# Two transformer layers and a gated block on one core: idle products at the start, modulation steps in other places, cross products of an inverse by halves

## The chip, the cores and the metric

The kernel runs on one core of a Trainium2 chip. The metric is the device time of one execution in microseconds; the kernel before has a median of 1013.92 over three runs (1012.06 to 1015.05). The engines are TensorE (PE, with its weight loads as PEld), VectorE (DVE), ScalarE (ACT), GpSimd (POOL) and SyncE (SP), which issues nearly all transfers.

## The reference, cut to what matters

Width 1024, 256 tokens, all in float32. A gated-linear-attention layer and an attention layer, each followed by a feed-forward with a convolution over three tokens, and then a block with a convolution branch, an RWKV-7 branch and a modulation by a vector c.

```python
def first_block(x, ...):
    for i in range(2):
        h = rmsnorm(x, norm_mix[i])
        x = x + (gla_mixer(h, ...) if i == 0 else attn_mixer(h, ...))
        x = x + conv_ffn(rmsnorm(x, norm_ffn[i]), w_up[i], w_conv[i], b_conv[i], w_down[i])
    return x

def gla_mixer(h, w_in, w_gate_up_f, ...):
    q, k, v, g, r = split(h @ w_in)                 # r: two ranks of 16 for the decays
    ...
    return (rmsnorm(o) * silu(g)) @ w_out

def conv_ffn(h, w_up, w_conv, b_conv, w_down):
    val, gate = split(depthwise_conv3(h @ w_up) + b_conv)
    return (silu(gate) * val) @ w_down

def second_block(x, c, ...):
    shift, scale, gate = split(silu(c) @ ada_w + ada_b)
    h = rmsnorm(x, norm_g) * (1 + scale) + shift
    c_val, c_gate, c_og, ts, r_og, g_conv, g_rwkv = split(h @ w_in)
    y_conv = silu(layernorm(conv31(c_val * sigmoid(c_gate)))) * silu(c_og) @ w_conv_out
    y_rwkv = rwkv7(ts, r_og)                        # state update by token, computed in chunks of 64
    m = sigmoid(g_conv) * y_conv + sigmoid(g_rwkv) * y_rwkv
    x = x + gate * (m @ w_out)
    return rmsnorm(x, final_g)
```

## The kernel before

Activations lie with the 1024 features on partitions, as 8 slices of 128 by 256 tokens. Each float32 matrix product is made of parts: ScalarE casts a weight slab of 128x1024 to its upper part hi (L78), VectorE subtracts it for the lower part lo (L80), and TensorE runs three products for each slice of 128 (mm3, L113 to L115), or one of width 512 over both parts of the activation and one of width 256 with the weight's lower part (mm2, L120 and L123). The weights come through SyncE's queue into a ring of five tiles `raw`; the tiles `adaw` of the modulation are in the same ring, so that a load waits until the tile five places earlier has been used up.

A list scheduler fixes each engine's order when the kernel is built; at run time an engine takes its instructions in that order and waits where an input is missing.

The stages are: gla (rank product `gr`, keys `pj`, queries, values, gates, output), ffn0, attn, ffn1 and second. The places that matter here:

- *Start.* `gla` makes the scaled activation (`ph_g`, `pl_g`), the rank product `gr` (64x256, eight slices), the column sums for the mean square (`rstd_cols`, L157, tile `nps_g`), then the key projection, four slabs of 24 products. `spread` (tile `rps_g`) brings the reciprocal root to all partitions. The products `lg` for the decays follow the keys. Ahead of all stand WARM products of 128x128 on ones (`warm`, L1331).
- *Modulation.* `ada` (L601) is a generator of 24 steps, eight for each third e of the modulation vector. One step loads 512 KB of `ada_w` into `adaw` and multiplies and adds it on VectorE into `ada` (L611, L613); the eighth also runs 16 small matmul rows `adaps` (L617) and an addition (L618). The table AD (L591) says how many steps are taken at each of the eight calls in gla (g), ffn0 (f0), attention (a) and ffn1 (f1).
- *Feed-forward.* For 22 pairs of slabs: up products, three-token convolution in `y` (L257 to L259), silu, product with the value (L263) and split into `gg` (ScalarE L130, VectorE L131). Then eight down products `dn` of 22 slices and their additions to x (L276).
- *Attention.* Keys are normed, turned (rope, L479 to L483) and transposed (`kTp`); queries follow; scores are reduced (mx, L568), exponentiated, scaled (rs, p, L574 and L577) and transposed (`pps`).
- *Inverse.* In `inv` the triangular inverse's diagonal blocks X are found by VectorE, which transposes them (X2 by halves at L869, all at L871); ScalarE copies the diagonal blocks into TT (L874); the cross blocks are products of 32x32, `zp` (L882) and `xp` (L892), copied at L885 and L895. `fill` puts products of other projections between them. Then `chain` follows the state over four chunks (`u`, `sp`, `op`).
- *End.* Conv branch: 31 taps on VectorE (L1081), normed into `yc`. `gated` projections give m and its parts `mh`; `wout` (L1122) multiplies by w_out with `project_both` and adds to x (L1131, twice for each slab, for the two parts of the activation); `final` (L1142) makes the last norm: squares on ScalarE, column sums, a square root that needs a table on ScalarE (loaded at L143), and four output pieces.

Of the kernel before, what the change touches and what calls it, by code (L numbers as in the profile page):

```python
# [10 lines left out]
F32 = mybir.dt.float32  # L11
# [6 lines left out]
P = 128  # L18
# [138 lines left out]
def rstd_cols(g, acc, name, eps=EPS):  # L157

    ps = g.ps.tile([P, 512], F32, name=f"nps_{name}")
    for t in range(2):  # L160
        for a in acc:
            g.nc.tensor.matmul(ps[:, 2 * t:2 * t + 2], a[:, t * P:(t + 1) * P], g.ones[:, :2], start=a is acc[0], stop=a is acc[-1])
    return rsqrt(g, ps[:, :4], 1.0 / D, eps, name)
# [134 lines left out]
def project(*a, **k):  # L298
    for _ in projecting(*a, **k):
        pass  # L300
# [45 lines left out]
def gla(g):  # L346
# [10 lines left out]
    for k in range(KD):  # L357
        mm3(nc, ps[:64, :T], (wh[:, k, :], wl[:, k, :]), (h[0][:, k, :], h[1][:, k, :]), k == 0, k == KD - 1)
    for d in range(2):
        rows = slice(32 * d, 32 * d + 16)  # L360
        nc.vector.tensor_tensor(out=rT[rows, :], in0=ps[rows, :T], in1=rstd[rows, :], op=ALU.mult)
# [229 lines left out]
AD = dict(zip(("g", "f0", "a", "f1"), "11111111,11111111,11111111,00000000".split(",")))  # L591
# [54 lines left out]
def second(g, order):  # L646
# [196 lines left out]
    def inv():  # L843
# [33 lines left out]
        for b in range(2):  # L877
            zp = psum.tile([P, 16, 32], F32, name=f"zp{b}")
            for i in range(16):
                for hf in range(2):  # L880
                    o = 64 * hf + 32
                    nc.tensor.matmul(zp[o:o + 32, i, :], Lb[64:96, hf, b, i, 32:], X2[64:96, hf, 16 * b + i, :], start=True, stop=True)  # L882
            for hf in range(2):
                o = 64 * hf + 32
                nc.scalar.copy(zt[o:o + 32, 16 * b:16 * b + 16, :], zp[o:o + 32])  # L885
            fill(1)
# [105 lines left out]
    def kept(name, src, f):  # L992
# [14 lines left out]
        def get(j):  # L1007
            t = sb.tile([P, T], F32, tag=name + "i", name=f"{name}i{j}")
            g.w.after(t, d[:, j, :])
            nc.scalar.activation(t, t, f)  # L1010
            return t
# [113 lines left out]
    def wout():  # L1125
        g.x = full("x2")
        g.w.after(g.x, g.xs)

        def ev(j, ps):
            for b in range(2):  # L1130
                nc.vector.scalar_tensor_tensor(out=g.x[:, j, :], in0=ps[:, b], scalar=g.mod[:, 16 + j:17 + j], in1=g.x[:, j, :], op0=ALU.mult, op1=ALU.add)  # L1131

        project_both(g, I["w_out"], v.mh, ev)
# [7 lines left out]
def final(g):  # L1141
# [8 lines left out]
    for a, n in ((0, 1), (1, 2), (3, 3), (6, 2)):  # L1150
# [144 lines left out]
def body(nc, tc, I, O, stages=("gla", "ffn0", "attn", "ffn1", "second")):  # L1295
    with ExitStack() as es:
# [33 lines left out]
        for _ in range(WARM):  # L1330
            nc.tensor.matmul(warm, g.ones, g.ones, start=True, stop=True)  # L1331
# [45 lines left out]
```

## Time and profile before

| | us |
|---|---|
| median of three runs | 1013.92 (1012.06 to 1015.05) |
| the profiled execution | 1013.54 |
| its span | 1011.7 |
| TensorE busy | 974.7 |
| VectorE busy | 832.3 |
| ScalarE busy | 611.0 |
| GpSimd busy | 5.1 |
| mean granted clock of TensorE | 0.983 |

The profile is of one execution. The span runs from its first to its last recorded instruction; 1.8 us of the profiled execution's time lie outside it. Busy times of engines overlap. Matmul ends are modelled: a product of width 256 is shown as about 0.28 us long although the next begins 0.12 us after it, so starts are read for the rate and not durations. The granted clock is a share of full speed, 2.4 GHz; the lower level, 1.2 GHz, shows as 0.5, and a stretch in between has held both.

### The profile page before, as it was taken

The page shows a single profiled execution, that of the slowest core. Times are in us where ns is not written, and L with a number is a line of the kernel's source. Part 1 is how long each engine was busy: PE and PEld are TensorE (multiplying, and loading weights), DVE is VectorE, ACT ScalarE, POOL GpSimd, SP SyncE. Part 2 cuts the span into 40 slices and gives each one's busy share as a digit, 9 for nine tenths or more (in the row PEclk, how much of TensorE's full clock was granted, in tenths as well). Part 3 has the DMA queues.
Part 4 walks back from the last instruction along what each step waited for, and adds up shares of the span by engine and source line. Part 5 has one row for each costly group of instructions (what it writes and reads, how often), then busy time and mean ns, then how long its engine had stood idle before and what let it go on. Part 6 is the DMA issues. An engine that isn't in the chain of part 4 may idle for free.

```text
span 1011.7 us, 19352 instructions
## 1 busy us (share of the span) xinstructions
PE 974.7 (96%) x7636; PEld 905.8 (90%) x7636; DVE 832.3 (82%) x1529; ACT 611.0 (60%) x1052; POOL 5.1 (0%) x15
## 2 busy tenths in 40 slices
PE   8999999999999999999999999999999999999796
PEld 7988899999888877999999889999988998898795
DVE  5956589888867886998888667999899898889795
ACT  6635666666544567676666456545676646745663
POOL 0000000000000000000000000000000000000000
PEclk8999999999999999999999999999999998999898
DMA  7738155556776861546656675455432362436451
GB/s 267 256 122 277 50 182 187 188 178 190 223 219 217 276 215 42 180 157 218 180 183 174 188 249 199 149 187 180 157 106 84 93 222 92 154 115 199 162 161 42
DMA packets 54442, 175.01 MB, mean 173 GB/s; under 512 B 6320, under 2 KB 12976, under 8 KB 53968
## 3 DMA queue, kind: packets, MB, share of 16 engines
q1 hardware_dynamic: 50464, 169.51, 52.7%
q10 hardware_dynamic: 3888, 4.27, 1.2%
q8 instruction: 60, 0.98, 0.4%
q14 instruction: 30, 0.25, 0.1%
HBM read 168.51 MB, written 5.24 MB: 172 GB/s over the span
## 4 chain that ended last, share of the span: by engine, by line
PE 79%; DVE 10%; DMA 4%; ACT 4%; issue 2%; ACTq 0%; DVEq 0%; SPq 0%
PE pj L113 8%; PE pj L115 8%; PE pj L114 8%; PE dn L120 8%; PE up L114 7%; PE up L115 7%; PE up L113 7%; PE pj L120 4%; PE dn L123 4%; DVE lo L80 3%; PE pj L123 2%; DMA adaw<-ada_w 2%; PE pt L113 2%; PE pt L114 2%; PE pt L115 2%
## 5 line engine op out<-in xcount | busy, mean ns | idle before, releaser
L78 ACT CAST hi<-raw 128x1024 fp32r<-128x1024 f32 (+2 forms) x286 | 295.0, 1034 | 243.2 <-PE pj L114 82.6
L80 DVE TENSOR_TENSOR lo<-raw,hi 128x1024 fp32r<-128x1024 f32 (+2 forms) x286 | 344.0, 1205 | 78.3 <-ACT hi L78 70.7
L114 PE MATMUL up<-h_f,hi 128*128 128x256 f32 x640 | 181.4, 284 | 0.5 <-DVE h_f L131 0.5
L113 PE MATMUL up<-h_f,hi 128*128 128x256 f32 x640 | 180.8, 283 | 0.3 <-ACT h_f L130 0.3
L115 PE MATMUL up<-h_f,lo 128*128 128x256 f32 x640 | 180.8, 283 | 0.0
L115 PE MATMUL pj<-h_s,lo 128*128 128x256 f32 x544 | 156.1, 287 | 1.7 <-DVE lo L80 1.7
L113 PE MATMUL pj<-h_s,hi 128*128 128x256 f32 x544 | 157.4, 290 | 0.0
L114 PE MATMUL pj<-h_s,hi 128*128 128x256 f32 x544 | 156.2, 287 | 0.0
L120 PE MATMUL dn<-gg,hi 128*128 128x512 f32 x352 | 124.9, 402 | 0.0
L114 PEld LDWEIGHTS up<-h_f,hi 128*128 128x128 f32 x640 | 122.8, 192 | 1.1 <-DVE h_f L131 1.1
L113 PEld LDWEIGHTS up<-h_f,hi 128*128 128x128 f32 x640 | 122.6, 192 | 0.5 <-ACT h_f L130 0.5
L115 PEld LDWEIGHTS up<-h_f,lo 128*128 128x128 f32 x640 | 122.8, 192 | 0.0
L115 PEld LDWEIGHTS pj<-h_s,lo 128*128 128x128 f32 x544 | 104.8, 193 | 2.6 <-DVE lo L80 1.9
L113 PEld LDWEIGHTS pj<-h_s,hi 128*128 128x128 f32 x544 | 104.9, 193 | 1.5
L114 PEld LDWEIGHTS pj<-h_s,hi 128*128 128x128 f32 x544 | 104.9, 193 | 1.1 <-issue 0.3
L1081 DVE SCALAR_TENSOR_TENSOR y<-u,long,y 128x233 f32<-128x233 f32 (+27 forms) x240 | 99.7, 469 | 0.7
L123 PE MATMUL dn<-gg,lo 128*128 128x256 f32 x352 | 97.1, 283 | 2.5 <-ACT gg L130 2.5
L120 PEld LDWEIGHTS dn<-gg,hi 128*128 128x128 f32 x352 | 66.2, 190 | 15.1
L123 PEld LDWEIGHTS dn<-gg,lo 128*128 128x128 f32 x352 | 67.0, 191 | 4.3 <-ACT gg L130 3.1
L257 ACT ACTIVATE y<-up,const 128x256 f32<-128x256 f32 x80 | 44.2, 556 | 1.9 <-DVE y L259 1.8
L259 DVE SCALAR_TENSOR_TENSOR y<-up,const,y 128x255 f32<-128x255 f32 x80 | 38.1, 479 | 1.2
L258 DVE SCALAR_TENSOR_TENSOR y<-up,const,y 128x255 f32<-128x255 f32 x80 | 37.9, 477 | 0.7 <-ACT y L257 0.7
(464 smaller groups left out, 1831.3 us busy)
## 6 DMA issues: line engine op xcount, KB each, us to landing
raw<-w_up SPq DMA_DIRECT2D x88, 512.0 KB, 4.1
raw<-w_down SPq DMA_DIRECT2D x32, 448.0 KB, 3.5
adaw<-ada_w SPq DMA_DIRECT2D x24, 512.0 KB, 4.5
raw<-w_down SPq DMA_DIRECT2D x16, 512.0 KB, 4.0
raw<-w_cvg SPq DMA_DIRECT2D x16, 512.0 KB, 4.1
raw<-gla_v SPq DMA_DIRECT2D x8, 512.0 KB, 5.1
raw<-gla_g SPq DMA_DIRECT2D x8, 512.0 KB, 3.7
raw<-gla_out SPq DMA_DIRECT2D x8, 512.0 KB, 4.8
```

What stands on the lines that cost most here:

```text
L78: nc.scalar.copy(hi[:, :w], raw[:, :w])
L80: nc.vector.tensor_tensor(out=lo[:, :w], in0=raw[:, :w], in1=hi[:, :w].bitcast(F32), op=ALU.subtract)
L113: nc.tensor.matmul(ps, lh, rh, start=start, stop=False)
L114: nc.tensor.matmul(ps, lh, rl, start=False, stop=False)
L115: nc.tensor.matmul(ps, ll, rh, start=False, stop=stop)
L120: wide = lambda: nc.tensor.matmul(ps, lhs[0], both, start=first, stop=last)
L123: nc.tensor.matmul(ps[:, 0], lhs[1], both[:, 0], start=False, stop=False)
L257: nc.scalar.activation(yb, ps[:, b, :], AF.Identity, scale=cw[:, 1, c:c + 1], bias=cw[:, 3, c:c + 1])
L258: nc.vector.scalar_tensor_tensor(out=yb[:, 1:], in0=ps[:, b, :T - 1], scalar=cw[:, 0, c:c + 1], in1=yb[:, 1:], op0=ALU.mult, op1=ALU.add)
L259: nc.vector.scalar_tensor_tensor(out=yb[:, :T - 1], in0=ps[:, b, 1:], scalar=cw[:, 2, c:c + 1], in1=yb[:, :T - 1], op0=ALU.mult, op1=ALU.add)
L1081: nc.vector.scalar_tensor_tensor(out=y[:, i:], in0=u[:, :T - i], scalar=w[:, j, 30 - i:31 - i], in1=y[:, i:], op0=ALU.mult, op1=ALU.add)
```

## The change

- `idle(n)` issues n products of 128x128 on ones into the `warm` tile. Besides the warm-up it is called in `gla` after each slice of the rank product: twice, and six times after the last.
- `rstd_cols` runs over the accumulators outside and the two halves of the tokens inside.
- AD: f0 loses its first two steps, f1 gets two (third and fourth call).
- `inv`: the cross products zp run for the first half over both banks, are copied, then for the second half; the calls of `fill` stand behind each half.
- `wout`: the square-root table is loaded on ScalarE behind the last sigmoid of a gate (`v.gate`); the last slab of w_out goes through `project` (three products of width 256 for each slice, one addition).
- `final`: the output in pieces of 1, 2, 2, 2, 1 slices.

```diff
@@ rstd_cols
-    for t in range(2):
-        for a in acc:
-            g.nc.tensor.matmul(ps[:, 2 * t:2 * t + 2], a[:, t * P:(t + 1) * P], g.ones[:, :2], start=a is acc[0], stop=a is acc[-1])
+    for a in acc:
+        for t in range(2):
+            g.nc.tensor.matmul(ps[:, 2 * t:2 * t + 2], a[:, t * P:(t + 1) * P], g.ones[:, :2], start=a is acc[0] and t == 0, stop=a is acc[-1], skip_group_check=True)
@@ gla
         mm3(nc, ps[:64, :T], (wh[:, k, :], wl[:, k, :]), (h[0][:, k, :], h[1][:, k, :]), k == 0, k == KD - 1)
+        g.idle(2 if k < KD - 1 else 6)
@@ AD
-AD = dict(zip(("g", "f0", "a", "f1"), "11111111,11111111,11111111,00000000".split(",")))
+AD = dict(zip(("g", "f0", "a", "f1"), "11111111,00111111,11111111,00110000".split(",")))
@@ inv
-        for b in range(2):
-            zp = psum.tile([P, 16, 32], F32, name=f"zp{b}")
-            for i in range(16):
-                for hf in range(2):
-                    o = 64 * hf + 32
-                    nc.tensor.matmul(zp[o:o + 32, i, :], Lb[64:96, hf, b, i, 32:], X2[64:96, hf, 16 * b + i, :], start=True, stop=True)
-            for hf in range(2):
-                o = 64 * hf + 32
-                nc.scalar.copy(zt[o:o + 32, 16 * b:16 * b + 16, :], zp[o:o + 32])
+        zp = [psum.tile([P, 16, 32], F32, name=f"zp{b}") for b in range(2)]
+        for hf in range(2):
+            o = 64 * hf + 32
+            for b in range(2):
+                for i in range(16):
+                    nc.tensor.matmul(zp[b][o:o + 32, i, :], Lb[64:96, hf, b, i, 32:], X2[64:96, hf, 16 * b + i, :], start=True, stop=True)
+                nc.scalar.copy(zt[o:o + 32, 16 * b:16 * b + 16, :], zp[b][o:o + 32])
             fill(1)
@@ second, get
-            nc.scalar.activation(t, t, f)
+            v.gate = nc.scalar.activation(t, t, f)
@@ wout
+        root_next(g, v.gate)
...
-        def ev(j, ps):
-            for b in range(2):
+        def ev(j, ps, n=2):
+            for b in range(n):
...
-        project_both(g, I["w_out"], v.mh, ev)
+        project_both(g, I["w_out"][:KD - 1], v.mh, ev)
+        project(g, I["w_out"][KD - 1:], (v.mh[:, 0], v.mh[:, 1]), lambda j, ps: ev(KD - 1, ps.unsqueeze(1), 1))
@@ final
-    for a, n in ((0, 1), (1, 2), (3, 3), (6, 2)):
+    for a, n in ((0, 1), (1, 2), (3, 2), (5, 2), (7, 1)):
@@ body
-        for _ in range(WARM):
-            nc.tensor.matmul(warm, g.ones, g.ones, start=True, stop=True)
+        def idle(n):
+            for _ in range(n):
+                nc.tensor.matmul(warm, g.ones, g.ones, start=True, stop=True)
+
+        g.idle = idle
+        idle(WARM)
```

What the scheduler makes of it is seen in the engines' orders. Names end in running numbers, which are 20 higher after the change at the start; `long` holds the ones, and lines after it are shifted by one to five.

TensorE at the start, behind the rank product, before (`pj_202` is the first key slab, `nps_g` the column sums):

```order
L113 MATMUL pj_202<-ph_g,hi_197 128x256
L114 MATMUL pj_202<-pl_g,hi_197 128x256
L115 MATMUL pj_202<-ph_g,lo_198 128x256
L162 MATMUL nps_g<-long,nacc_g 128x2
L162 MATMUL nps_g<-long,sq_g_144 128x2
L162 MATMUL nps_g<-long,nacc_g 128x2
L162 MATMUL nps_g<-long,sq_g_144 128x2
L113 MATMUL pj_202<-ph_g,hi_197 128x256
```

The same place after:

```order
L115 MATMUL gr<-ph_g,lo_98 64x256
L1333 MATMUL warm<-long 128x128 x2
L162 MATMUL nps_g<-long,nacc_g 128x2 x2
L162 MATMUL nps_g<-long,sq_g_144 128x2 x2
L1333 MATMUL warm<-long 128x128 x4
L113 MATMUL pj_222<-ph_g,hi_217 128x256
L114 MATMUL pj_222<-pl_g,hi_217 128x256
L115 MATMUL pj_222<-ph_g,lo_218 128x256
```

The column sums now stand ahead of every key product, the first key slab (now `pj_222`) behind four of the idle ones; two idle ones follow each slice of the rank product, the last of these seen here.

VectorE at the end of ffn0, before (`ada` the modulation step, `sg_21` and `gg` the last gated tile, `dn_0` the first down product):

```order
L259 SCALAR_TENSOR_TENSOR y_0_21_2972<-up_21_2911,const_1258,y_0_21_2972 128x255
L80 TENSOR_TENSOR lo_3103<-raw_3101,hi_3102 128x896
L258 SCALAR_TENSOR_TENSOR y_0_21_2976<-up_21_2911,const_1258,y_0_21_2976 128x255
L259 SCALAR_TENSOR_TENSOR y_0_21_2976<-up_21_2911,const_1258,y_0_21_2976 128x255
L613 SCALAR_TENSOR_TENSOR ada_2987<-adaw_3_3192,long,ada_2987 128x1024
L263 TENSOR_TENSOR sg_21_2980<-sg_21_2980,y_0_21_2972 128x256
L131 TENSOR_TENSOR gg_1352<-sg_21_2980,gg_1352 128x256
L276 TENSOR_TENSOR x<-dn_0_2986,x 128x256
```

The same place after:

```order
L80 TENSOR_TENSOR lo_3096<-raw_3094,hi_3095 128x896
L258 SCALAR_TENSOR_TENSOR y_0_21_2996<-up_21_2931,const_1278,y_0_21_2996 128x255
L259 SCALAR_TENSOR_TENSOR y_0_21_2996<-up_21_2931,const_1278,y_0_21_2996 128x255
L80 TENSOR_TENSOR lo_3116<-raw_3114,hi_3115 128x896
L263 TENSOR_TENSOR sg_21_3000<-sg_21_3000,y_0_21_2992 128x256
L131 TENSOR_TENSOR gg_1372<-sg_21_3000,gg_1372 128x256
L614 SCALAR_TENSOR_TENSOR ada_3137<-adaw_1_3206,long,ada_3137 128x1024
```

The step at the gated tile now follows it; before it stood ahead.

VectorE at the end of ffn1, before:

```order
L258 SCALAR_TENSOR_TENSOR y_1_21_6130<-up_21_6065,const_3541,y_1_21_6130 128x255
L259 SCALAR_TENSOR_TENSOR y_1_21_6130<-up_21_6065,const_3541,y_1_21_6130 128x255
L80 TENSOR_TENSOR lo_6250<-raw_6248,hi_6249 128x896
L263 TENSOR_TENSOR sg_21_6134<-sg_21_6134,y_1_21_6126 128x256
L131 TENSOR_TENSOR gg_4506<-sg_21_6134,gg_4506 128x256
L276 TENSOR_TENSOR x<-dn_0_6140,x 128x256 x2
```

The same place after (`adaw_7` belongs to the last step of the last third, e2):

```order
L259 SCALAR_TENSOR_TENSOR y_1_21_6134<-up_21_6069,const_3545,y_1_21_6134 128x255
L80 TENSOR_TENSOR lo_6254<-raw_6252,hi_6253 128x896
L263 TENSOR_TENSOR sg_21_6138<-sg_21_6138,y_1_21_6130 128x256
L614 SCALAR_TENSOR_TENSOR ada_3924<-adaw_7_6343,long,ada_3924 128x1024
L131 TENSOR_TENSOR gg_4510<-sg_21_6138,gg_4510 128x256
L276 TENSOR_TENSOR x<-dn_0_6144,x 128x256 x2
```

A step now stands between the product with the value (L263) and the lower part of the last gated tile (L131).

## Rows read from the trace of the kernel before

**Rows 1.** Page, part 1: TensorE's busy time, share of the span, instructions.

```profile
PE 974.7 (96%) x7636; PEld 905.8 (90%) x7636; DVE 832.3 (82%) x1529; ACT 611.0 (60%) x1052; POOL 5.1 (0%) x15
```

**Rows 2.** TensorE by windows: length, busy (instructions), granted clock, DMA share, GB/s.

```profile
10.00:20.00 10.00, 7.89 (x41) 0.69 0.88 312
...
276.00:286.00 10.00, 7.45 (x34) 0.83 0.52 151
...
840.00:850.00 10.00, 8.89 (x156) 0.67 0.16 40
```

**Rows 3.** Timeline, TensorE, start: start us, us, line, operation, [idle before <-releaser].

```profile
11.70 0.38 PE L113 MATMUL pj<-ph_g,hi 128*128 128x256 f32 x1 [1.27 <-ACT hi L78]
...
13.04 0.39 PE L115 MATMUL pj<-ph_g,lo 128*128 128x256 f32 x1 [0.84 <-DVE lo L80]
...
15.99 0.41 PE L114 MATMUL pj<-pl_g,hi 128*128 128x256 f32 x1
...
22.14 0.60 PE L170 MATMUL rps_g<-long,r_g 128*128 128x128 f32 x4
...
29.15 1.99 PE L377 MATMUL lg<-const,rT 17*128 17x512 f32 x8
```

**Rows 4.** Timeline, VectorE, the same stretch.

```profile
12.90 0.95 DVE L187 TENSOR_TENSOR nacc_g<-nacc_g,sq_g 128x256 f32<-128x256 f32 x2
...
19.28 1.23 DVE L80 TENSOR_TENSOR lo<-raw,hi 128x1024 fp32r<-128x1024 f32 x1 [2.16 <-PE pj L115]
```

**Rows 5.** Timeline, VectorE, end of the first feed-forward.

```profile
277.27 1.28 DVE L613 SCALAR_TENSOR_TENSOR ada<-adaw,long,ada 128x1024 f32<-128x1024 f32 x1 [2.71 <-DMA adaw<-ada_w]
...
286.27 0.88 DVE L276 TENSOR_TENSOR x<-dn,x 128x256 f32<-128x256 f32 x2 [0.54 <-PE dn L120]
```

**Rows 6.** Timeline, first down products on TensorE, second feed-forward's end on VectorE.

```profile
266.19 0.40 PE L120 MATMUL dn<-gg,hi 128*128 128x512 f32 x1
...
547.79 0.40 PE L120 MATMUL dn<-gg,hi 128*128 128x512 f32 x1
...
551.84 1.09 DVE L80 TENSOR_TENSOR lo<-raw,hi 128x896 fp32r<-128x896 f32 x1
...
563.58 0.89 DVE L276 TENSOR_TENSOR x<-dn,x 128x256 f32<-128x256 f32 x2 [0.48 <-PE dn L120]
```

**Rows 7.** DMA issues, 262 to 290: KB each, median us to landing.

```profile
adaw<-ada_w SPq DMA_DIRECT2D x3, 512.0 KB, 4.8
```

**Rows 8.** Timeline, TensorE, end of the first feed-forward.

```profile
324.94 1.84 PE L617 MATMUL adaps<-long,ada 128*128 128x2 f32 x16
```

**Rows 9.** Timeline, attention, TensorE and then VectorE.

```profile
355.34 0.30 PE L531 MATMUL kTp<-long,akr 128*128 128x128 f32 x1 [1.52 <-DVE akr L483]
...
380.78 0.17 DVE L574 RECIPROCAL rs<-rs 128x2 f32<-128x2 f32 x1 [1.65 <-ACT p L573]
```

**Rows 10.** Timeline, second block's inverse and convolution: TensorE, VectorE, TensorE.

```profile
842.68 3.19 PE L882 MATMUL zp<-X,VU 32*32 32x32 f32 x124 [0.59 <-DVE X L869]
...
852.52 2.21 PE L892 MATMUL xp<-TT,X 32*32 32x32 f32 x126
...
861.10 0.69 DVE L650 TENSOR_TENSOR S<-sp,long 128x512 f32<-128x512 f32 x1 [3.46 <-PE sp L924]
...
950.44 0.80 PE L113 MATMUL pj<-yc,hi 128*128 128x256 f32 x2 [3.52 <-ACT yc L130]
```

**Rows 11.** Timeline, last projection and final norm: ScalarE, VectorE, TensorE.

```profile
974.58 0.42 ACT L1010 ACTIVATE gci<-gci 128x256 f32<-128x256 f32 x1 [1.39 <-DMA gci<-gcd]
...
1001.85 1.28 ACT L143 ACT_TABLE_LOAD   x1
...
979.51 0.42 DVE L131 TENSOR_TENSOR mh<-m,mh 128x256 fp32r<-128x256 f32 x1
...
999.98 1.00 DVE L1131 SCALAR_TENSOR_TENSOR x<-pj,long,x 128x256 f32<-128x256 f32 x2 [0.51 <-PE pj L120]
...
979.51 0.40 PE L123 MATMUL pj<-mh,lo 128*128 128x256 f32 x2
```

## The prediction

> **What bounds the kernel now.** I read the page's busy times first: TensorE works 974.7 of 1011.7 us [rows 1], so the sum of its work and of its waits is the span, and an edit is worth something only if it shortens TensorE's work, its waits or the time in which its clock is down. Then the stretches: the granted clock is 0.69 in 10 to 20 us, 0.83 in 276 to 286 and 0.67 in 840 to 850 [rows 2], and in each of them TensorE had just stood idle. The timeline of each place gave what it waited for: casts at the start [rows 3], a modulation step queued on VectorE at the end of the first feed-forward [rows 5], VectorE's transposes in the inverse [rows 10]. Differences between two like stretches (the ends of the two feed-forwards) price an edit best, because they hold idle time and low clock together.
>
> The profiled execution took 1013.54 us (span 1011.7), 0.38 below the median of 1013.92; the sum is made on 1013.54. A measurement of this kernel can tell about 0.3% (3.0 us) from no change.
>
> **The start.** Before, TensorE waits 1.27 and 0.84 us for the first weight's halves, then runs nine products, the column sums and the rest, with products of 0.41 us at the low clock; the last of the four key tiles is done when lg begins, at 29.15 [rows 3]. After, two idle products follow each step of the rank product and the rest stand behind the column sums, so that no key product runs before these. One 128x128 product on ones costs at most 0.60/2 = 0.30 us, from rps_g [rows 3]. Fourteen of them stretch the rank product by 3 to 4 us, which fill the two waits; the sums' last input is ready at 12.90 + 0.95 = 13.85 [rows 4], four sums and four idle products at some 0.23 each (0.30 less the tail that the next one covers) take 1.8: key products begin near 15.7. Ninety-six, 0.12 apart as products of this width are at full clock, with rps_g's 0.6 end at 27.8, and somewhat earlier if part of the last input's wait is covered. VectorE's weight subtraction at 19.28, which waited 2.16 us for TensorE [rows 4], finds a free buffer earlier in the new order, so the reciprocal behind it comes in time. I take **-1.5**. If the clock falls all the same, the nine early products are lost (1.1) and four idle ones run slowly (0.2 more): +1.3. Ends: -2.2 and +1.3.
>
> **The modulation steps.** Of e1's eight steps in f0 six remain; its last two go to the head of attention, and e2's last two move from attention to f1.
> *End of f0.* VectorE's step at 277.27 waited 2.71 us for its weights and stood ahead of the last gated tile [rows 5], for which TensorE waited. From the first down product to the last pair of additions it is 286.27 - 266.19 = 20.08 us; in f1, which has no steps, 563.58 - 547.79 = 15.79 [rows 5, 6]. After, the step there stands behind the gated tile; e1's first step stands among the convolution of the tile before, for weights asked for two loads earlier. The difference is 4.29; I keep 0.14 for that step: **-4.15** (ends -4.3 and -3.0).
> *f0's adaps* (1.84 us of TensorE [rows 8]) leave the end of f0, but VectorE has constants, additions and sums due there, so that I count **-0.75** (0 to -1.84).
> *Attention.* The 1.52 us that TensorE waits for the keys [rows 9] shrink, as fewer steps stand before them; a whole adaps (1.84 [rows 8]) comes earlier and another leaves; four steps of 1.28 us (the length in [rows 5]) now stand among the softmax operations, where VectorE had gaps such as 1.65 [rows 9]. Between -1.0 (the keys' wait gone, steps in the gaps) and +3.5 (5.1 less the one gap) I take **+0.6**, near the lower end, since before had two steps in the same place.
> *f1.* One adaps more: **+1.84** [rows 8]. Its second step is queued on VectorE directly ahead of the last gated tile. Its weights can be asked for only when the weight five before has been used, at 551.84 + 1.09 = 552.9 [rows 6], and land 4.8 us later by the median of f0's [rows 7], 4.3 if they do as the faster ones: 557.2, step until 558.5, gated tile 558.9. The order lets TensorE do 57 products, 28.5 pairs at (563.58 - 547.79)/44 = 0.36 us, before the wide product that needs it: 547.79 + 10.2 = 558.0 [rows 6]. Stall **+0.9**; 0.3 if the weights land sooner, 4.29 if it costs what it cost in f0, low clock included.
>
> **The inverse.** Of the 128 cross rows only four ran ahead; TensorE waited 0.59 us for the second transpose, then ran 124 in 3.19 us [rows 10]. After, 64 run ahead, ScalarE's four copies come before its copies of the transposes instead of around them, and the state product comes earlier, for which VectorE stands 3.46 us [rows 10]. TensorE gains of this only what VectorE's convolution, now ahead, shortens later: the 3.52 us it waits for yc [rows 10], because products are then left to cover that chain. I take **-1.8**, half of the 3.46 (ends -0.3 and -3.5).
> What a run of 32 products on one array tile costs, where the two tiles alternated, no row shows. The nearest: xp's alternating 126 rows in 2.21 us, 17.5 ns each, and from above adaps, one tile throughout but the whole array, 1.84/16 = 115 ns each [rows 8, 10]. I take xp's, the same shape; 115 is the slow rival below.
> The Trainium skill, "TensorEngine Tiling (Array Packing)", Key Properties, says that different tiles can load weights and multiply in parallel; by that the old alternation overlaps and the new runs cannot, which speaks against this edit. Taken as a doubling of 26 ns for 128 rows it would add 3.3 us, and the sum below would be 1011.9 instead of 1008.6; no row of before shows one tile alone in this shape, so the trace does not settle it.
>
> **The ends.** In the column sums two products instead of three follow the last input: **-0.2** over the seams that wait for them (0 to -0.6). The square-root table, loaded at 1001.85 for 1.28 us [rows 11], is loaded behind the last gate's sigmoid at 974.58 instead: of the load only what outlasts the mean's way to VectorE was exposed, so -0.6. But there it delays the cast at ScalarE that follows, with it VectorE's half of the last mh slice (done 979.9), which TensorE takes at once, at 979.5 to 980 [rows 11]: +1.2 (0 if other products cover it). The last slab of w_out as one product of width 256 per step needs one addition of 0.5 where two took 1.00 [rows 11]: -0.5. The output in five pieces with a smaller last: 0, plus or minus one such operation of 0.5. Together **+0.1** (-1.6 to +1.3).
>
> **Sum.** -1.5 - 4.15 - 0.75 + 0.6 + 1.84 + 0.9 - 1.8 - 0.2 + 0.1 = -4.96; 1013.54 - 4.96 = **1008.6 us**.
>
> **The rivals.**
> *The step ahead of the tile moves, not goes.* f1's step costs what f0's cost (4.29 for 0.9, +3.4), and the four steps in the softmax cost 3.5 for 0.6 (+2.9): 1008.6 + 6.3 = **1014.9**, slower than before. It is one mechanism, VectorE's queue held by a step on which TensorE does not depend, in f1 and attention; it decides once both together cost 5 us more than I count. For it: the same order did exactly this at 277.27 [rows 5]. Against it: one step, not several, is late in f1, and attention had gaps.
> *The clock falls at the start anyway.* TensorE stays busy on ones, but a few waits remain: +1.3 for -1.5, **1011.4**. For it: 1.27 and 0.84 us sufficed [rows 3]. Against: both are filled.
> *One array tile is slow.* 128 rows at 115 ns are 14.7 us where some 3.4 stood: +11.3, and the inverse's -1.8 is lost: **1021.7**. From 39 ns more a row (5 us) the change is no gain at all. For it: adaps [rows 8]. Against: its weights are 128 columns wide, these 32. The doubling of 26 ns that the parallel tiles suggest gives **1011.9**.
> *More than counted.* The clock holds in the inverse (0.67 over 840 to 850 [rows 2] loses 3.3 us), the softmax's steps fall in gaps and the new adaps are covered: -1.7, -1.6, -1.8: **1003.5**.
>
> **How the numbers follow.** Chances: forecast 0.57 (1005.5 to 1010.9), steps ahead of the tile 0.11, clock at the start 0.10, doubled tile 0.06, slow tile 0.03, more than counted 0.13. Faster by over 0.3% is under 1010.9: forecast 0.57, more 0.13, a third of the clock case 0.03, of the steps' case 0.02: 0.75. Slower is over 1017: the slow tile 0.03, a part of the steps' case 0.03: 0.06. The rest is 0.19. The range of 1003.5 to 1014 leaves out about 0.07 below (half of the last case) and 0.11 above.
>
> **What would show it.** After: clock near 1.00 in 10 to 30 us and lg at 27 to 28 from the start; from the first down product of f0 to its last additions under 17 us; f1's the same stretch 18 to 19, with VectorE waiting for adaw there; VectorE's wait for the state product under 2 us and the wait for yc shorter by 1 to 3; no table load after 1000, but a wait of about 1 us near the first slab of w_out. A low clock after 15 us, f1's stretch over 20, cross rows over 40 ns, or a wait over 2 us in the softmax would prove a step wrong.

## The result and the profile after

The changed kernel takes 1022.53 us (median of four), before 1014.48; the ratio of the two is 1.0077, 95% interval 1.0060 to 1.0094. It is slower by 0.8%, where 1008.6 and a gain were forecast. One of the four executions (1069.72, mean granted clock 0.836) and one of the ten of f1_after_two below (1032.16) were in a slower state, which the medians hold and the ratios leave out. The profiled execution of the changed kernel took 1021.69 us, span 1019.8. The page's first part:

```profile
PE 979.5 (96%) x7684; PEld 910.4 (89%) x7684; DVE 831.9 (82%) x1529; ACT 611.1 (60%) x1052; POOL 4.8 (0%) x15
```

TensorE is busy for 4.8 us more than in [rows 1], slow stretches included; the other 3.4 us of the span are waits. Where the 8.16 us of the span come from is best read by following the start of one and the same TensorE instruction through both traces:

| TensorE instruction | before, us | after, us | difference | won or lost since the row above |
|---|---|---|---|---|
| first lg | 29.15 | 28.06 | -1.09 | -1.09 |
| first nps_a (end of ffn0) | 334.36 | 328.04 | -6.31 | -5.22 |
| last pps (attention) | 401.16 | 395.54 | -5.62 | +0.69 |
| last dn (ffn1) | 609.78 | 606.55 | -3.23 | +2.39 |
| first kbp | 753.45 | 750.21 | -3.25 | 0.0 |
| last nl | 798.03 | 796.33 | -1.70 | +1.55 |
| first zp | 840.52 | 842.83 | +2.31 | +4.01 |
| last zp | 845.64 | 851.74 | +6.10 | +3.79 |
| last cmean | 932.49 | 939.85 | +7.36 | +1.26 |
| last pj from yc | 977.04 | 983.93 | +6.89 | -0.47 |
| end of span | 1011.7 | 1019.8 | +8.16 | +1.27 |

Up to 753 us the change does nearly what was forecast (-3.25; the terms for the start, f0, its adaps, attention and f1 add up to -3.06, with the column sums to -3.26; but two of these terms are off by nearly the same amount in opposite directions, as the account point by point shows). Then three stretches lose 9.4 us: a fall of the clock, the wait before the cross products zp, and these products themselves.

TensorE by windows (length, busy and instructions, granted clock, DMA share, GB/s):

```profile
10.00:20.00 10.00, 9.90 (x85) 1.00 0.89 322
276.00:286.00 10.00, 10.00 (x59) 1.00 0.66 209
840.00:850.00 10.00, 7.17 (x102) 0.57 0.22 71
850.00:860.00 10.00, 10.00 (x217) 0.75 0.17 54
```

Against [rows 2]: the first two windows have the full clock now, and the inverse is worse, 0.57 for 0.67; the low clock lasts into the window behind it (0.75, where the trace of before has 0.99).

The start, on TensorE (start us, us, line, operation, instructions, idle before and its releaser):

```profile
14.93 1.14 PE L1333 MATMUL warm<-long 128*128 128x128 f32 x8
...
19.27 0.71 PE L170 MATMUL rps_g<-long,r_g 128*128 128x128 f32 x4
...
28.06 1.13 PE L378 MATMUL lg<-const,rT 17*128 17x512 f32 x4
```

The last idle products (x8, so four of them) end with the clock up, and lg comes at 28.06 for 29.15 in [rows 3].

The ends of the two feed-forwards, TensorE and then VectorE:

```profile
265.04 0.40 PE L120 MATMUL dn<-gg,hi 128*128 128x512 f32 x1
...
542.18 0.40 PE L120 MATMUL dn<-gg,hi 128*128 128x512 f32 x1
...
553.10 0.72 PE L120 MATMUL dn<-gg,hi 128*128 128x512 f32 x2 [0.45 <-DVE gg L131]
```

```profile
274.50 1.28 DVE L614 SCALAR_TENSOR_TENSOR ada<-adaw,long,ada 128x1024 f32<-128x1024 f32 x1 [0.64 <-DMA adaw<-ada_w]
...
280.83 0.88 DVE L276 TENSOR_TENSOR x<-dn,x 128x256 f32<-128x256 f32 x2 [0.48 <-PE dn L120]
...
551.42 1.28 DVE L614 SCALAR_TENSOR_TENSOR ada<-adaw,long,ada 128x1024 f32<-128x1024 f32 x1 [1.45 <-DMA adaw<-ada_w]
552.63 0.42 DVE L131 TENSOR_TENSOR gg<-sg,gg 128x256 fp32r<-128x256 f32 x1
...
558.84 0.88 DVE L276 TENSOR_TENSOR x<-dn,x 128x256 f32<-128x256 f32 x2 [0.47 <-PE dn L120]
```

In f0 the step at 274.50 stands behind the gated tile, and from the first down product to the second pair of additions it is 280.83 - 265.04 = 15.79 us, where [rows 5, 6] gave 20.08. In f1 the step waits 1.45 us for its weights, the gated tile behind it comes at 552.63, TensorE waits 0.45 for it, and the same stretch is 558.84 - 542.18 = 16.66 for 15.79.

The stretch before the inverse, ScalarE of the changed kernel:

```profile
825.69 0.37 ACT L1003 COPY scogo<-pj 128x256 f32<-128x256 f32 x1 [2.99 <-DMA scogd<-scogo]
...
826.54 1.05 ACT L78 CAST hi<-raw 128x1024 fp32r<-128x1024 f32 x1 [0.47 <-ACT scogo L1003]
830.26 0.37 ACT L1003 COPY scogo<-pj 128x256 f32<-128x256 f32 x1 [2.67 <-PE pj L115]
...
838.31 0.37 ACT L1003 COPY gro<-pj 128x256 f32<-128x256 f32 x1 [2.21 <-DMA grd<-gro]
```

and ScalarE of the kernel before, its longest waits of this kind there:

```profile
831.19 0.37 ACT L1004 COPY gro<-pj 128x256 f32<-128x256 f32 x1 [1.15 <-DMA scogd<-scogo]
...
836.99 0.37 ACT L1004 COPY gro<-pj 128x256 f32<-128x256 f32 x1 [1.19 <-DMA grd<-gro]
```

These copies bring projections from PSUM to SBUF (L1003 after, L1004 before), from where each is written to DRAM (scogd, grd). They now wait 2 to 3 us for a write. (The trace puts the wait of 2.67 us at 830.26 down to TensorE, but the products that this copy takes were done by 825.4; in e3_start_ad below the same copy's wait is put down to the write.) The casts (L78) stand behind them on ScalarE, and VectorE's subtractions behind the casts; on VectorE the steps of the inverse are queued behind those:

```profile
827.62 1.22 DVE L80 TENSOR_TENSOR lo<-raw,hi 128x1024 fp32r<-128x1024 f32 x1 [2.02 <-ACT hi L78]
...
832.54 1.23 DVE L80 TENSOR_TENSOR lo<-raw,hi 128x1024 fp32r<-128x1024 f32 x1 [1.77 <-ACT hi L78]
```

In the kernel before VectorE has no wait over 0.25 us between 800 and 842. 2.02 and 1.77 us make up 3.8 of the 4.0 by which the first zp is late. Then TensorE, in the inverse and at yc:

```profile
842.83 3.59 PE L883 MATMUL zp<-X,VU 32*32 32x32 f32 x64 [5.25 <-DVE X L870]
...
847.71 1.91 PE L883 MATMUL zp<-X,VU 32*32 32x32 f32 x32
...
850.07 1.91 PE L883 MATMUL zp<-X,VU 32*32 32x32 f32 x32
...
957.80 0.58 PE L113 MATMUL pj<-yc,hi 128*128 128x256 f32 x1 [3.52 <-ACT yc L130]
```

TensorE waits 5.25 us for the transposes, then 64 zp rows take 3.59 us and twice 32 take 1.91, 56 to 60 ns a row; in [rows 10] it was 124 in 3.19, 26 ns. (A row is one record of the trace; each of the 64 products zp shows as two. The length of a run holds the modelled end of its last row, 0.19 to 0.24 us; from start to start a row of the changed kernel takes 53 ns. The 26 ns are a mean over both levels of the clock, 16 and then 27 from start to start.) The wait for yc is 3.52 us, as in [rows 10]. VectorE's wait for the state product, 3.46 us in [rows 10], is longer:

```profile
865.68 0.69 DVE L651 TENSOR_TENSOR S<-sp,long 128x512 f32<-128x512 f32 x1 [7.15 <-PE sp L923]
```

The end, ScalarE and then TensorE:

```profile
983.13 1.28 ACT L154 ACT_TABLE_LOAD   x1
```

```profile
987.12 0.50 PE L120 MATMUL pj<-mh,hi 128*128 128x512 f32 x1 [0.79 <-DVE mh L131]
...
988.35 0.38 PE L123 MATMUL pj<-mh,lo 128*128 128x256 f32 x1 [0.61 <-ACT mh L130]
...
989.39 0.50 PE L120 MATMUL pj<-mh,hi 128*128 128x512 f32 x1 [0.41 <-DVE mh L131]
```

The table load stands between the last gate and the cast, and TensorE waits 0.79 + 0.61 + 0.41 = 1.81 us in the first slab of w_out. From the last products of w_out (+9.50) to the end of the span (+8.16) 1.3 us come back.

### The profile page after: what moved, and what is told of

It reads as the page before. It is cut to its first block, busy times and chain, and to the rows that moved or that the text cites. A ratio compares the mean times of both kernels' runs of the same rounds, so it can differ in the third digit from the quotient of the medians.

```text
span 1019.8 us, 19438 instructions
## 1 busy us (share of the span) xinstructions
PE 979.5 (96%) x7684; PEld 910.4 (89%) x7684; DVE 831.9 (82%) x1529; ACT 611.1 (60%) x1052; POOL 4.8 (0%) x15
## 4 chain that ended last, share of the span: by engine, by line
PE 53%; DVE 7%; ACT 3%; DMA 2%; issue 1%; DVEq 0%; ACTq 0%; SPq 0%
PE pj L114 7%; PE pj L113 7%; PE pj L115 7%; PE up L114 4%; PE up L115 4%; PE up L113 4%; PE dn L120 3%; PE pj L120 2%; DVE lo L80 2%; PE dn L123 2%; PE pj L123 1%; DMA scogi<-scogd 1%; ACT hi L78 1%; PE pt L113 1%; PE pt L115 1%
## 5 line engine op out<-in xcount | busy, mean ns | idle before, releaser
L78 ACT CAST hi<-raw 128x1024 fp32r<-128x1024 f32 (+2 forms) x286 | 295.0, 1034 | 237.9 <-PE pj L114 78.7
L1080 DVE SCALAR_TENSOR_TENSOR y<-u,long,y 128x235 f32<-128x235 f32 (+24 forms) x240 | 99.5, 463 | 0.9
L614 DVE SCALAR_TENSOR_TENSOR ada<-adaw,long,ada 128x1024 f32<-128x1024 f32 x21 | 26.9, 1281 | 15.8 <-DMA adaw<-ada_w 15.8
L259 DVE SCALAR_TENSOR_TENSOR y<-up,const,y 128x255 f32<-128x255 f32 x80 | 38.1, 479 | 1.2
```

Source lines behind the costliest of these rows:

```text
L78: nc.scalar.copy(hi[:, :w], raw[:, :w])
L259: nc.vector.scalar_tensor_tensor(out=yb[:, :T - 1], in0=ps[:, b, 1:], scalar=cw[:, 2, c:c + 1], in1=yb[:, :T - 1], op0=ALU.mult, op1=ALU.add)
L614: nc.vector.scalar_tensor_tensor(out=acc, in0=r, scalar=sc[:, k:k + 1], in1=acc, op0=ALU.mult, op1=ALU.add)
L1080: nc.vector.scalar_tensor_tensor(out=y[:, i:], in0=u[:, :T - i], scalar=w[:, j, 30 - i:31 - i], in1=y[:, i:], op0=ALU.mult, op1=ALU.add)
```

## The experiments

Every ratio is to the kernel before on the same chip. The last columns are from the profiled executions: how far each stands ahead of (-) or behind (+) the one of before at three instructions and at the end. One execution has a scatter of its own: e2_inv_only is 0.76 behind at 747 us, where it has no change yet. The profiled executions of e1_inv_old (1013.6) and f1_after_two (1012.0) are the fastest of their kernels, those of g1_start (1021.5) and f2_before_one (1026.3) the slowest.

| kernel | median us | ratio (95%) | last vt, 747 | first zp | last zp | end |
|---|---|---|---|---|---|---|
| changed kernel | 1022.53 | 1.0077 (1.0060 to 1.0094) | -3.24 | +2.31 | +6.10 | +8.16 |
| e1_inv_old | 1018.27 | 1.0061 (1.0036 to 1.0085) | -3.21 | +0.91 | +1.74 | +0.08 |
| e2_inv_only | 1020.08 | 1.0070 (1.0043 to 1.0098) | +0.76 | +1.45 | +5.12 | +6.46 |
| e3_start_ad | 1017.37 | 1.0039 (1.0021 to 1.0057) | -1.25 | +2.37 | +3.20 | +2.99 |
| e4_no_root | 1015.41 | 1.0030 (1.0009 to 1.0051) | -3.77 | +1.47 | +2.29 | +1.50 |
| f1_after_two | 1017.81 | 1.0042 (1.0008 to 1.0076) | -3.65 | -3.58 | -1.79 | -1.85 |
| f2_before_one | 1024.36 | 1.0100 (1.0054 to 1.0146) | -0.02 | +4.40 | +5.23 | +12.87 |
| f3_best | 1009.82 | 0.9967 (0.9953 to 0.9981) | -2.17 | -2.21 | -3.14 | -3.56 |
| f4_same_tile | 1014.91 | 1.0025 (0.9996 to 1.0055) | -0.50 | -0.52 | +0.27 | +0.75 |
| g1_start | 1017.54 | 1.0041 (1.0021 to 1.0060) | +0.11 | +6.92 | +7.75 | +8.09 |
| g2_start_two | 1012.20 | 0.9992 (0.9973 to 1.0011) | -2.44 | -0.91 | -0.64 | -1.49 |
| g3_ad | 1012.20 | 0.9995 (0.9974 to 1.0017) | -2.01 | -2.03 | -2.02 | -2.34 |
| g4_steps_later | 1011.62 | 0.9986 (0.9964 to 1.0008) | -2.24 | -2.24 | -1.84 | -2.16 |

### The inverse taken back, and the inverse alone

e1_inv_old is the changed kernel with the loops of before in `inv`:

```diff
-        zp = [psum.tile([P, 16, 32], F32, name=f"zp{b}") for b in range(2)]
-        for hf in range(2):
-            o = 64 * hf + 32
-            for b in range(2):
-                for i in range(16):
+        for b in range(2):
+            zp = psum.tile([P, 16, 32], F32, name=f"zp{b}")
+            for i in range(16):
+                for hf in range(2):
+                    o = 64 * hf + 32
```

> The changed kernel with the inverse of before. Theory A (the inverse's new order costs the time: runs of products on one array tile, 30 us per thousand rows more, and the late start that goes with it): the zp rows fall from 60 to about 26 ns each, TensorE's wait before them from 5.25 to about 1.3 us, and the time from 1022.5 to 1013 to 1014.5. Theory B (the late start comes from spill writes that land later, whatever the inverse does): zp rows at 26 ns, but the wait of 4 to 5 us stays, 1017 to 1019. Theory C (the losses lie in the end and in clock falls elsewhere): 1020 or more.

e2_inv_only is the kernel before with the new loops (the same lines with the signs turned).

> The kernel before with the new inverse alone. Theory A: 1014.5 + 8 = 1022 or so, zp rows near 60 ns and the wait ahead of them 4 to 5 us. Theory B: only the rows' price, 128 x 34 ns = 4.4 us, less at most 1 us of earlier copies: 1018 to 1019, wait ahead of zp near 1.3 us. If the step of my prediction stood (the order gains 1.8): 1012.7.

Neither theory comes out whole. With the old inverse the wait before zp stays: between 747 us and the first zp that kernel loses 4.1 us, like the changed one, and 1018.27 is what theory B gave. With the new inverse alone hardly anything is lost before the first zp (0.7), but the zp rows cost what they cost in the changed kernel. TensorE in e2_inv_only:

```profile
841.97 3.46 PE L882 MATMUL zp<-X,VU 32*32 32x32 f32 x64 [1.98 <-DVE X L869]
...
846.73 1.91 PE L882 MATMUL zp<-X,VU 32*32 32x32 f32 x32
```

From the first to the last zp it loses 3.7 us, and 1.3 more by the end. So there are two losses: the rows, which the inverse brings, and the late start, which comes with one of the other parts.

### The start and the steps alone, and the early table load taken out

e3_start_ad is the kernel before with `idle`, its calls in `gla`, and the new AD.

> The kernel before with the idle products at the start and the new places of the modulation steps alone. Both theories of the inverse expect what the trace of the changed kernel shows up to 744 us, -3.2: 1011.3. Theory B adds that a shift of 3 us alone can bring the late spill write: then 1015, with a wait of 4 us or more before zp.

It is 1.25 us ahead at 747 and loses 3.6 us from there to the first zp, without any change in the inverse or behind it. ScalarE of e3_start_ad:

```profile
825.20 0.37 ACT L1005 COPY scogo<-pj 128x256 f32<-128x256 f32 x1 [2.08 <-DMA scogd<-scogo]
...
830.41 0.37 ACT L1005 COPY scogo<-pj 128x256 f32<-128x256 f32 x1 [3.32 <-DMA scogd<-scogo]
```

The late start is here, and in no part of the code that was changed. That it is 1.25 and not 3.2 ahead at 747 lies in the seam to attention: with the old order of the column sums its keys come 7.1 us early, in the changed kernel 8.8, and a low clock at 333 us falls into it (granted clock 0.77, shown at the end).

e4_no_root is e1_inv_old without this line:

```diff
     def wout():
-        root_next(g, v.gate)
         g.x = full("x2")
```

> The changed kernel with the inverse of before and without the early load of the square-root table; the last slab through the plain projection stays. If the early load costs what its trace shows (TensorE waits 0.79 + 0.61 + 0.41 in the first slab of w_out, against 0.6 us saved at the end): about 1.2 us below the kernel that differs only in that load. If the last slab's new form is what costs: the same as that kernel.

From the last product of yc to the end of the span e4_no_root wins 0.08 us (+1.58 to +1.50) and e1_inv_old, with the load, 0.27 (+0.35 to +0.08): in these two executions the load returns what it costs. But in the first slab of w_out the three profiles with the load and the new last slab lose 2.6, 1.0 and 2.1 us (changed kernel, e1_inv_old, f1_after_two), the three without it 0.4, 0.7 and 1.2 (e4_no_root, f3_best, g4_steps_later); between the last products of w_out and `rps_final` those with it gain 1.4 us, those without 0.6. The load returns 0.8 us, and what it costs varies by more than that. The medians, 1015.4 and 1018.3, differ in the direction of the 1.2 us expected, but the intervals of the two ratios overlap: whether the load loses is not settled.

### Where the spill copies go

The program that was built lists the address of every tile in SBUF; the eight copies scogo and the first two of gro, in order:

```
before        219776 226944 219776 226944 219776 226944 219776 226944 | 219776 226944
changed       214656 137856 214656 214656 214656 214656 214656 214656 | 217728 214656
e2_inv_only   219776 226944 219776 226944 219776 226944 219776 226944 | 219776 226944
e3_start_ad   214656 137856 214656 214656 214656 214656 214656 214656 | 217728 214656
```

The code asks for two tiles in turn (tag "spill", bufs=2). In the changed kernel seven of the eight scogo fall on one address, the last six without a break (the six of the expectations below), so that a copy has to wait for the write of the copy just before, not of the one before that. Two kernels put the tiles by hand, f1_after_two in the changed kernel and f2_before_one, with one tile in place of two (`range(1)` and `j % 1` in the lines below), in the kernel before:

```diff
     v = Ctx()
+    v.spl = None
...
-            t = sb.tile([P, T], F32, tag="spill", bufs=2, name=f"{name}o{j}")
+            if v.spl is None:
+                v.spl = [sb.tile([P, T], F32, name=f"spl{i}_") for i in range(2)]
+            t = v.spl[j % 2]
             nc.scalar.copy(t, ps)
```

> The changed kernel, whose spill copies go by hand to two fixed tiles in turn. In the built program of the changed kernel six of the eight copies scogo lie at one address, in that of before they alternate between two. Theory D (the idle products move the tiles that are placed later, the spill copies lose their second tile, ScalarE waits at each copy for the write just before, and the casts and VectorE's inverse behind them come late): ScalarE's waits for scogd and grd of 2 to 3 us go back to about 1, TensorE's wait before zp from 5.25 to 1.3, and the time from 1022 to about 1018. Theory E (writes land late because the shift brings them together with weight loads): waits and time stay.

> The kernel before, whose spill copies all go to one tile; nothing else differs. Theory D: ScalarE waits 2 to 3 us for the write just before, twice or more between 818 and 842, TensorE waits 4 to 5 us before zp, and the time rises by about 4 us, to 1017. Theory E: no change, 1013.

Theory D holds both ways. In f1_after_two nothing is lost between 747 us and the first zp (-3.65 to -3.58), and the median falls from 1022.5 to 1017.8. In the changed kernel the writes themselves were not slow: between 813 and 842 us those of scogo landed 3.4 us after their issue (median), in the kernel before 4.1. f2_before_one, which is the kernel before in all but this, shows the waits (ScalarE, then TensorE):

```profile
826.53 0.37 ACT L1007 COPY spl__8949<-pj 128x256 f32<-128x256 f32 x1 [2.17 <-DMA scogd<-spl__8949]
...
832.44 0.37 ACT L1007 COPY spl__8949<-pj 128x256 f32<-128x256 f32 x1 [4.01 <-DMA scogd<-spl__8949]
```

```profile
844.92 0.42 PE L883 MATMUL zp<-X,VU 32*32 32x32 f32 x4 [5.68 <-DVE X L870]
...
847.49 3.62 PE L883 MATMUL zp<-X,VU 32*32 32x32 f32 x124
```

TensorE waits 5.68 us before zp and the kernel is at 1.0100, more than the 4 us expected: another 7.6 us come behind the inverse (+5.23 at the last zp, +12.8 forty us later), where one more such copy waits 5.67 us for a write and the granted clock is 0.66 from 880 to 890 (0.83 before).

Which part moves the tiles was asked with the idle products alone, g1_start, and with the same on two fixed tiles, g2_start_two:

```diff
         mm3(nc, ps[:64, :T], (wh[:, k, :], wl[:, k, :]), (h[0][:, k, :], h[1][:, k, :]), k == 0, k == KD - 1)
+        g.idle(2 if k < KD - 1 else 6)
```

> The kernel before with the idle products alone. In its built program the spill copies stand as in the changed kernel, six of the eight scogo at one address. Theory D: 1.1 us ahead until 798 us by the clock kept at the start, then ScalarE waits 2 to 3 us for scogd and TensorE 4 to 5 before zp; 3 us or more behind at the end, 1016 to 1017. If the move of the modulation steps is what moves the tiles: no such waits, 1012.

> The kernel before with the idle products alone, and the spill copies by hand on two fixed tiles. Theory D: only the start's gain is left, 1.1 to 1.5 us: 1011.7. If idle products cost by something other than the copies: the same as the kernel without the fixed tiles.

g1_start has the addresses of the changed kernel and its waits, on ScalarE and, before zp, on TensorE:

```profile
828.47 0.37 ACT L1005 COPY scogo<-pj 128x256 f32<-128x256 f32 x1 [2.41 <-DMA scogd<-scogo]
...
834.95 0.37 ACT L1005 COPY scogo<-pj 128x256 f32<-128x256 f32 x1 [4.58 <-DMA scogd<-scogo]
```

```profile
847.44 0.42 PE L883 MATMUL zp<-X,VU 32*32 32x32 f32 x4 [6.51 <-DVE X L870]
```

6.8 us are lost between 747 and the first zp, 1.55 of them by a fall of the clock at 767 us and 5.3 by the wait, and the kernel is slower by 0.4%; with the fixed tiles the idle products alone are no slower than before (0.9992). So the idle products, at 7 to 16 us, cost their price at 825 us, through the places that the tiles get when the program is built. How the allocator comes from twenty more products in an early PSUM tile to other places 800 us later was not followed further.

The move of the steps alone has the addresses of before:

> The kernel before with the modulation steps in their new places alone; the spill copies alternate as before. By the trace of the changed kernel: 4 us ahead at the end of f0, 4.5 to 7 in attention, 2.4 given back in f1 (adaps 1.84 and a wait of 0.5), 2 to 2.5 ahead at the end: 1010.5 to 1011.

It is 2.0 us ahead from ffn1 on and stays so through the inverse; 0.9995 and 1012.2 are less than the 2.3 us of its profiled execution would give, and within what can be told from no change.

### The price of a row on one tile

f4_same_tile is the kernel before with two loops turned, inside each bank:

```diff
         for b in range(2):
             zp = psum.tile([P, 16, 32], F32, name=f"zp{b}")
-            for i in range(16):
-                for hf in range(2):
+            for hf in range(2):
+                for i in range(16):
```

> The kernel before, in whose inverse the 16 products zp of one half follow each other and then those of the other half, inside each bank; copies and fills stay. If products on one array tile cannot overlap: a zp row takes 56 to 60 ns at the low clock where it took 26, the 124 rows 7 us where they took 3.2, and the time rises by 3 to 4 us. If the price in the changed kernel came from the gaps around them: 26 ns and no change.

TensorE of f4_same_tile:

```profile
840.00 2.21 PE L882 MATMUL zp<-X,VU 32*32 32x32 f32 x64 [1.24 <-DVE X L869]
...
842.81 3.34 PE L882 MATMUL zp<-X,VU 32*32 32x32 f32 x64
```

and of f1_after_two, where the halves follow each other as in the changed kernel:

```profile
836.95 2.18 PE L884 MATMUL zp<-X,VU 32*32 32x32 f32 x64 [1.33 <-DVE X L871]
...
839.84 1.90 PE L884 MATMUL zp<-X,VU 32*32 32x32 f32 x32
...
842.18 1.91 PE L884 MATMUL zp<-X,VU 32*32 32x32 f32 x32
```

The first 64 rows of both, all on one tile of the array, run at the full clock: 2.21 and 2.18 us, from start to start 32 ns a row. In turn, at the full clock, f3_best's TensorE has

```profile
838.32 0.31 PE L884 MATMUL zp<-X,VU 32*32 32x32 f32 x4 [1.24 <-DVE X L871]
...
840.49 2.21 PE L884 MATMUL zp<-X,VU 32*32 32x32 f32 x124 [0.60 <-DVE X L871]
```

2.21 us for 124, from start to start 16 ns, as xp in [rows 10]. Where all products of a run stay on one tile a row takes twice as long as where the products alternate. At the low clock it is 53 ns for 27. The kernel itself is 1.0025, interval 0.9996 to 1.0055: +0.8 us from the first to the last zp in its trace, less than the 3 to 4 expected: its first 64 ran at the full clock, and the 0.59 us that TensorE waited for the second transpose are gone.

### A version that is faster than both

f3_best has the idle products, the new AD, the column sums, the last slab by the plain projection and the five output pieces; it leaves out the new inverse and the early table load, and has the two fixed tiles.

> Idle products, modulation steps, column sums, last slab and output pieces of the changed kernel, the inverse of before, no early table load, and two fixed tiles for the spill copies. Theory D with the inverse as the second loss: up to zp 3.8 us ahead of before, as the parts' traces have it, and at the end 3.5 to 4.5 ahead: 1008.5 to 1009.5. Theory E: 1013 or more, as the kernel that differs only in the tiles measured 1015.4.

1009.82 us, 0.9967 with interval 0.9953 to 0.9981: faster than before by 0.3% and, by the two ratios, than the changed kernel by 1.1%. At the first zp it is 2.2 us ahead where 3.8 was expected, at the end 3.6. e4_no_root differs from it in the two fixed tiles alone and stands at 1.0030, with an interval of 1.0009 to 1.0051 that lies apart: the places of the tiles are worth 0.6% here.

By the ratios the two losses are larger than in the single traces. The places cost 0.5% (g1_start against g2_start_two), 0.6% (e4_no_root against f3_best) and 1.0% (f2_before_one); the new inverse costs 0.7% alone, and 0.8% with the load between f3_best and f1_after_two. Either is more than the 0.3% that the other parts gain, so that with only one of the two taken back the changed kernel stays slower than before: 1.0061 without the new inverse, 1.0042 with the fixed tiles.

g4_steps_later differs from f3_best in the last entry of AD only, "00001100":

> The best version so far (1009.8), with the two steps of f1 at its fifth and sixth call instead of the third and fourth; on VectorE they then stand behind the last gated tile. The wait of 0.45 us for that tile goes and the 1.84 of adaps stays: f1 from its first down product to the last additions 15.8 + 1.84 = 17.7 us where it took 18.2, and 1009.3. If the steps there hold up additions that TensorE waits for: 1010 or more.

On VectorE the steps now stand behind the last gated tile, and the wait of TensorE for that tile goes: from its first to its last down product f1 takes 63.37 us, in f3_best 64.16. But f1 begins 0.7 us later than there, so that the last dn stands where it stood (-2.26 for -2.18 us), and 1011.62 (0.9986) is not better. What cost the 0.7 us ahead of f1 these runs do not show.

## Why the prediction was wrong, point by point

- **The start**: forecast -1.5, measured -1.09 (28.06 for 29.15). Mechanism and clock as forecast. What failed is the step that summed its cost at the start alone. No term, end or rival of the prediction asked what the edit does to the places of tiles later on, and it cost 4.0 us there (5.3 in g1_start alone): ScalarE's copies wait for their own writes, and VectorE's inverse comes late. Of my rivals none held this; the nearest to its sign, a step that holds a queue, was another mechanism.
- **The steps in f0**: forecast -4.15 and, for the adaps, -0.75, together -4.90; measured -5.22 up to the first column sum of attention, -4.29 of it to the second additions. Right.
- **Attention**: +0.6 forecast, +0.69 measured, but the agreement is luck. The two kernels with the moved steps and the old order of the column sums (e3_start_ad, g3_ad) lose 2.53 and 2.59 us between the first nps_a and the last pps; the six with the moved steps and the new order lose 0.69 to 0.96. The steps cost 2.5 there, within the ends given, and the column sums give most of it back. **f1**: +2.74 forecast, +2.39 measured, of it 0.87 in the stretch to the second additions (0.9 forecast). f1 is right, and the rival in which the step moves its price to f1 did not come.
- **The inverse**: forecast -1.8; it is a loss. The step that failed is the one that took xp's 17.5 ns for a row on one tile because the shape was the same. xp's rows alternate between tiles; the rule of the Trainium skill that I weighed there, "TensorEngine Tiling (Array Packing)", Key Properties (different tiles work in parallel), speaks of this difference, and the runs agree with it: 32 ns against 16 at the full clock. I gave it 0.06. It came out as a doubling at either level of the clock, 53 ns against 27 at the low one; behind the wait of 5.25 us all rows ran at the low one, where in f1_after_two, behind a wait of 1.33 us, the first 64 ran at the full one. The second half of that step failed too: the wait for yc stayed 3.52 us, so nothing that VectorE gained came through, and VectorE's wait for the state product, forecast under 2 us, rose to 7.15. Between f1_after_two and f3_best, which have like places of tiles, the new inverse (with the load at the end) costs 3.1 us from the last nl to the last product of yc in the profiled executions; the medians of the two are 8.0 us apart, at mean granted clocks of 0.968 to 0.990 and 0.984 to 0.991, and the profile of f1_after_two is its fastest.
- **The column sums**: -0.2 forecast (0 to -0.6), about -1.8 in the seam ahead of attention. From the first nps_a to the keys the six kernels with the moved steps and the new order gain 2.4 to 2.9 us, the two with the old order 0.6 and 0.7. TensorE of the changed kernel, then of e3_start_ad (g3_ad has 0.76 there, the other five with the new order 1.00):

```profile
330.00:335.00 5.00, 3.90 (x20) 1.00 0.91 294
```

```profile
330.00:335.00 5.00, 3.66 (x15) 0.77 0.90 299
335.00:340.00 5.00, 5.00 (x21) 0.89 0.55 154
```

  The term was mis-sized: it counted products that follow the last input and left out the clock, which falls there with the old order and not with the new one. 0.23 and 0.11 of 5 us each are 1.7 us.
- **The end**: +0.1 forecast; +1.27 in the changed kernel's profile, -0.27 and -0.08 in those of e1_inv_old and e4_no_root, +0.2 in f3_best. All are within the ends that were given. The load returns 0.8 us at the square root, for 0.6 forecast; its cost, forecast 1.2, is not settled (1.81 us of waits in the changed kernel).
- **The clock at 767 us**: +1.55 in the changed kernel, with the same waits of 0.7 to 0.9 us ahead of it as before. It fell there in the profiles of e4_no_root, g1_start and g2_start_two too, and in none of the other ten. What decides it stays open.
- **The range**, 1003.5 to 1014, had its upper end from known parts. In the profiled execution the two mis-steps, 4.0 and 3.8 us at zp, with the 1.55 of the clock, carry the time from the -3.25 that came as forecast in sum to +6.1.

## What to carry to other kernels

An edit to a kernel whose tiles are placed by an allocator can change the waits in stages that it does not touch: compare the places, or the waits, of the reused tiles in both programs before costing an edit as local, and give staging tiles that must alternate a place by hand. Small products on parts of the array cost by their neighbours: keep rows on different tiles in turn, or price the run by a row that really stays on one tile. Where a wait is followed by such small work, the clock can make it dearer still: 53 ns a row behind the wait of 5.25 us, 32 at the full clock. Where an edit has several parts, take back more than one at a time too: here either loss alone kept the kernel slow.

## What was not expected of the hardware

A 32x32 row in a run on one part of the array took 32 ns at the full clock and 53 ns at the low one, with two parts in turn 16 and 27 ns. A copy from PSUM whose SBUF tile was still being written out waited 2 to 5.7 us for a write of 128 KB, while weight loads of 512 KB were under way. And a wait of 5.25 us before the inverse left the granted clock at 0.57 and 0.75 in the twenty us from 840, where it had been 0.67 and 0.99 after waits of 1.25 and 0.59.
